# Two transformer blocks on one core: the attention heads and the second block's projections issued in a written order, and one PSUM bank for each branch product

## The chip, the cores and the metric

One core of a Trainium2 chip runs the whole program. Its engines work side by side from queues of their own: PE (TensorE, matrix products into PSUM), DVE (VectorE), ACT (ScalarE), POOL (GpSimd), and SP, which issues the transfers. The metric is the device time of one execution in microseconds (us), as the median of several.

## The reference

The input is one sequence of 256 tokens of width 1024, and everything is float32. The first model has two layers, each with a SwiGLU feed-forward, a mixer, and another feed-forward. The mixer of the second layer is a differential attention with 8 heads, whose keys and values come from the end of the first layer:

```python
    k, v = jnp.split(rms_norm(x, g_kv) @ w_kv, 2, axis=-1)
    ...
    q = (h @ w_q).reshape(b, s, N_HEADS, 2, HEAD_DIM) * (HEAD_DIM ** -0.5)
    ...
        scores = jnp.einsum("bqhcd,bkhcd->bhcqk", qb, k).astype(f32)
        ...
        p = jax.nn.softmax(jnp.where(causal, scores, -jnp.inf), axis=-1)
        a = p[:, :, 0] - lam * p[:, :, 1]
        return jnp.einsum("bhqk,bkhe->bqhe", a.astype(v.dtype), v)
    ...
    o = rms_norm(o, g_subln) * (1.0 - lambda_init)
    return o.reshape(b, s, D_MODEL) @ w_o
```

A second model follows. From the normalised tokens it projects the operands of two mixers: an HGRN2 recurrence with chunks of 64, and a sparse attention with rotary positions whose keys and values are compressed (32 tokens at a stride of 16, plus a position term, through a small two-layer network) and also used directly. The outputs of the two mixers are each multiplied by a branch weight and gated, added, and projected; a last feed-forward ends the program.

## The kernel before

**Precision and weights.** Each float32 operand is split into a high part and a remainder, so that one product is three matmuls (high by high, low by high, high by low). The weights arrive as 1 MB chunks in three `raw` buffers; the class `Stream` makes of each half chunk a high part (`hi()`, an ACT copy, line 194) and a remainder (`lo()`, a DVE subtraction, line 207) in ten pairs of slots `wh`, `wl`. `pump()` is one `hi` and one `lo`; `take` hands out halves in order; `done` frees a slot when its last matmul has been issued. Every matmul goes through the helper at line 430.

**Order.** Inside `with ordered():` the instructions of each engine stand in the order in which the code issues them. Outside it a scheduler chooses the order by priorities. Every engine works through its own instructions one after the other.

**PSUM.** `ps("acc")` has four banks of 128x512 float32, `ps("mm")` two and `ps("tr")` two.

**Ends of a feed-forward.** `Tail.close` accumulates the down projection, and between its rows it issues the next norm: `c2` the sum of squares, `c3a` and `c3b` the scaling (line 369) whose result PE transposes (line 416), and `fill`, the transposes and their splitting (lines 420 and 421). `close(ahead=2)` is that of the output projection of the attention, `close()` with `ahead=0` that of five other stages.

**Attention, 694 to 768 us.** For each head the scheduler gets: `att_kq` (k piece and q piece of 24 matmuls each, two `pump`s, two ACT copies to `kq`), `att_T(h-2)` (three transposes of the softmax result and one ACT copy, line 972), `att_scores(h)`, `att_av(h-2)` (three products with v into a `tr` bank, two ACT squares, then `rov` on DVE, a power on POOL, and the scaled result `gain` on DVE, line 988), and `att_soft(h)`. The last is on DVE two mask additions (line 944), which stand for `dg` in the texts, and four maxima (line 952); then four exponentials on ACT (line 955); then on DVE a reciprocal and five small products (lines 957 to 963), called the combination below. `v_part(1, 0)` and `v_part(1, 1)`, each 24 matmuls of 512 columns, stand ahead of heads 5 and 6. `att_out(pr)` transposes two heads' `gain` on PE (line 999) for the output projection `wo`, whose rows `wo.row` of six matmuls each stand in a written order from 768 us on, with the last heads' work between them.

**Projections of the second block, 992 to 1032 us.** `proj` is a product of 24 matmuls and one ACT copy (line 1086); `rope` is six small DVE operations; `dup_T` is two DVE copies (line 1111) and four transposes of their result. The sums of the compression (line 1153) read the transposed tokens `cT` and write `fT`, which the first product of `cmp_hidden` reads.

**Branch products, 1167 to 1186 us.** Eight products go to `acc` banks, two to each bank, and DVE multiplies each by its gate (line 1561).

Of the kernel before, what the change touches and what calls it, by code (L numbers as in the profile page):

```python
# [19 lines left out]
P = 128  # L20
T = 256
# [219 lines left out]
def tile_model(ctx: ExitStack, tc: tile.TileContext, w, wkv, x_in, gains, cst_in, pos_in, lbp, out):  # L241
# [334 lines left out]
    class Tail:  # L576
# [19 lines left out]
        def close(self, at=None, ahead=0):  # L596
# [5 lines left out]
            with ordered():  # L602
                for i in range(at, n):
                    self.row(0, i)
                self.row(1, rows[0])
                st.hi()
                bd.c2(0)
                bd.c3a(0)
                bd.c3b(0)
                for i in rows[1:5]:  # L610
                    self.row(1, i)
                    if i < rows[4]:
                        st.hi()
                st.lo()
                st.lo()
                bd.fill(0)
                for i in rows[5:-1]:
                    st.hi()
                    self.row(1, i)
                st.lo()  # L620
                st.lo()
                self.row(1, n - 1)
                bd.c2(1)
                bd.c3a(1)
                bd.c3b(1)
                while st.lo():
                    pass
# [283 lines left out]
    with ordered():  # L911
        v_part(0, 0)
        v_part(0, 1, {3: lambda: b4.fill(1)})
# [5 lines left out]
    def att_kq(h):  # L919
# [3 lines left out]
        st.pump(1)  # L923
        ws_piece(o[:, 1], ch, 1, qx)
        st.done(ch)
        kq = sb([P, 2, T], "opair", bufs=2)
        nc.scalar.activation(kq[:, 0], o[:, 0], AF.Copy)
        nc.scalar.activation(kq[:, 1], o[:, 1], AF.Copy, scale=0.125)
        st.pump(1)
        return kq  # L930

    def att_scores(h, kq):
# [73 lines left out]
    for h in range(8):  # L1006
        if h in (5, 6):
            v_part(1, h - 5)
        kq = att_kq(h)
        if h == 7:  # L1010
            att_out(0)
            att_out(1)
            b5.prep()
        if h >= 2:
            att_T(h - 2)
        sc = att_scores(h, kq)
        if h >= 2:
            att_av(h - 2)
        aa[h] = att_soft(h, sc)
# [16 lines left out]
    with ordered():  # L1036
        wo.row(0, 0)
        att_out(2)
        outs(2)
        wo.row(0, 1)  # L1040
        att_T(6)
# [46 lines left out]
    with ordered():  # L1088
        ch_1 = st.take(2)
        proj(bq[:, 0, 512:908], 0, ch_1, 396)  # L1090
        ch_q = st.take(2)
        proj(bq[:, 0, 0:512], 0, ch_q, 512, {5: lambda: b6.fill(1)})
        st.pump(2)
        proj(bq[:, 1, 512:908], 1, ch_1, 396)
        finish(ch_1)
        proj(bq[:, 1, 0:512], 1, ch_q, 512)
        finish(ch_q)
    ch_2 = st.take(2)
    for tb in range(2):
        rope(hd[:, tb, 0:10], tb, [P, 10, 8])  # L1100
        proj(bq[:, tb, 908:], tb, ch_2, 396)
    finish(ch_2)

# [13 lines left out]
    for tb in range(2):  # L1117
        rope(hd[:, tb, 12:20].rearrange("p (a b) d -> p a b d", b=4)[:, :, 0:2], tb, [P, 2, 2, 8])
    for tb in range(2):
        cs = slice(tb * P, (tb + 1) * P)  # L1120
        pt = ps("tr")
        for j in range(4):
            nc.tensor.transpose(pt[:, j * P:(j + 1) * P], bq[:, tb, j * P:(j + 1) * P], ident)
        pv = hv(pt)
        for i in range(2):
            nc.scalar.activation(qk_t[i][:, :, cs], pv[:, 2 * i:2 * i + 2], AF.Copy, scale=0.125)

    gates = sb([P, 2, 24], "gates")
    af = sb([P, 2, 512], "tmp", bufs=2)
    ch_f = st.take(2)  # L1130
    proj(af[:, 0], 0, ch_f, 512)
    for tb in range(2):
        cs = slice(tb * P, (tb + 1) * P)
        pv = dup_T(tb, (12, 16))
        for i in range(2):
            nc.scalar.activation(qk_t[2 + i][:, :, cs], pv[:, 2 * i:2 * i + 2], AF.Copy)
    proj(af[:, 1], 1, ch_f, 512)
    finish(ch_f)
    for tb in range(2):
        cs = slice(tb * P, (tb + 1) * P)  # L1140
        nc.scalar.activation(cT[:, :, cs], dup_T(tb, (8, 10)), AF.Copy)
    nc.scalar.activation(gates, bq[:, :, 1280:], AF.Sigmoid)
    nc.scalar.activation(af, af, AF.Sigmoid)
    ff = sb([P, D], "gain", bufs=2)
    fT = ff[:, :960].rearrange("p (s j g n) -> p s j g n", s=2, j=16, g=2)
    nc.gpsimd.memset(ff[:, 960:], 0.0)
    cv = cT.rearrange("p (s g) (n j e) -> p s j e g n", s=2, n=16, e=2)
    for s in range(2):
        for e in range(2):
            r = slice(e * 64, e * 64 + 64)  # L1150
            for hf in range(2):
                for g in range(2):
                    nc.vector.tensor_tensor(
                        fT[r, s, hf * 8:hf * 8 + 8, g],
                        cv[r, s, :, e, g, hf:hf + 15],
                        pe[r, s, hf * 8:hf * 8 + 8, None].to_broadcast([64, 8, 15]), op=OP.add)
# [603 lines left out]
```

## Time and profile before

| what | value |
|---|---|
| median of 3 runs | 1413.23 us (1412.24 to 1414.88) |
| the profiled execution's own time | 1413.44 us |
| its span, first to last instruction | 1411.4 us |
| mean granted clock of TensorE | 0.995 |
| PE busy | 1386.1 us (98%) |
| DVE busy | 873.3 us (62%) |
| ACT busy | 732.1 us (52%) |

The time of the execution holds 2.0 us outside the span. [...] A row of the timeline gives the start, the length, the instruction with its tiles (written <- read), how many were joined in the row, and in brackets how long the engine had been idle before it, with the instruction that ended the wait. Lengths of matmuls overlap in the pipeline, so the distance of two starts is what a matmul costs.

### The profile page before, as it was taken

What the parts mean: (1) busy time and instruction counts of PE and PEld (TensorE: products, weight loads), DVE (VectorE), ACT (ScalarE), POOL (GpSimd) and SP (SyncE); (2) the same over time, 40 slices, a digit from 0 to 9 for tenths busy, and PEclk for the clock granted to TensorE, in tenths of its full rate; (3) what the DMA queues carried; (4) which work ended last, traced back from release to release, by engine and by line L of the source; (5) the groups of instructions that cost most, each with busy time, mean ns of one, the idle gap of its engine ahead of it and who ended that gap; (6) DMA issues with size and microseconds to landing.
All of it is one profiled execution on the core that took longest, in us unless ns stands there. A gap on an engine that the chain in (4) does not pass through costs nothing.

```text
span 1411.4 us, 23060 instructions
## 1 busy us (share of the span) xinstructions
PE 1386.1 (98%) x9533; PEld 1268.7 (90%) x9533; DVE 873.3 (62%) x1358; ACT 732.1 (52%) x1216; POOL 32.3 (2%) x55
## 2 busy tenths in 40 slices
PE   8999999999999999999999999999999998999998
PEld 7999989999999899998898899998867998899996
DVE  5565576876555575654876765555679556675552
ACT  5454455455444454543665554444476954464451
POOL 0000000000000000000000000000000000000000
PEclk9999999999999999999999999999999999999999
DMA  7554556456555465554443465553653334355540
GB/s 272 204 201 179 185 226 216 176 183 222 196 179 179 151 237 184 208 191 150 154 175 134 151 246 186 183 186 112 234 228 120 120 135 161 123 211 207 183 146 30
DMA packets 38361, 252.93 MB, mean 179 GB/s; under 512 B 4328, under 2 KB 4720, under 8 KB 9968
## 3 DMA queue, kind: packets, MB, share of 16 engines
q1 hardware_dynamic: 37232, 250.20, 49.2%
q8 instruction: 75, 1.23, 0.3%
q10 hardware_dynamic: 1024, 1.25, 0.2%
q14 instruction: 30, 0.25, 0.0%
HBM read 250.39 MB, written 1.05 MB: 178 GB/s over the span
## 4 chain that ended last, share of the span: by engine, by line
PE 89%; DVE 5%; ACT 3%; issue 1%; DMA 1%; POOL 0%; ACTq 0%; POOLq 0%; DVEq 0%
PE mm L430 57%; PE acc L430 28%; PE tr L430 2%; DVE wl L207 2%; ACT wh L194 1%; PE tr L416 1%; PE tr L1300 0%; DVE x L351 0%; ACT junk L318 0%; DMA cst<-in_cst_dram 0%; POOL ssr L329 0%; DMA raw<-in_w_dram 0%; PE tr L554 0%; DVE tmp L340 0%; DVE ev L720 0%
## 5 line engine op out<-in xcount | busy, mean ns | idle before, releaser
L207 DVE TENSOR_TENSOR wl<-raw,wh 128x1024 fp32r<-128x1024 f32 (+1 forms) x454 | 539.6, 1213 | 189.4 <-ACT wh L194 186.3
L194 ACT ACTIVATE wh<-raw 128x1024 fp32r<-128x1024 f32 (+1 forms) x454 | 462.6, 1047 | 163.8 <-PE mm L430 87.8
L430 PE MATMUL mm<-xth,wh 128*128 128x256 f32 x1728 | 490.0, 284 | 0.6 <-DVE ev L1543 0.5
L430 PE MATMUL mm<-xth,wl 128*128 128x256 f32 x1728 | 487.8, 282 | 0.0
L430 PE MATMUL mm<-xtl,wh 128*128 128x256 f32 x1728 | 487.1, 282 | 0.0
L430 PE MATMUL acc<-wh,h 128*128 128x512 f32 x1120 | 352.7, 396 | 0.0
L430 PEld LDWEIGHTS mm<-xth,wh 128*128 128x128 f32 x1728 | 325.6, 188 | 3.3 <-DVE ev L1543 0.7
L430 PEld LDWEIGHTS mm<-xtl,wh 128*128 128x128 f32 x1728 | 326.0, 189 | 2.3 <-issue 0.5
L430 PEld LDWEIGHTS mm<-xth,wl 128*128 128x128 f32 x1728 | 325.2, 188 | 0.6 <-issue 0.5
L430 PEld LDWEIGHTS acc<-wh,h 128*128 128x128 f32 x1120 | 206.9, 188 | 46.1
L430 PE MATMUL acc<-wl,h 128*128 128x512 f32 x560 | 221.3, 395 | 0.0
L430 PE MATMUL mm<-wh,xth 128*128 128x256 f32 (+2 forms) x496 | 158.4, 319 | 1.9 <-ACT wh L194 1.7
L430 PE MATMUL mm<-wl,xth 128*128 128x256 f32 (+2 forms) x496 | 156.2, 315 | 1.6 <-DVE wl L207 1.4
L430 PE MATMUL mm<-wh,xtl 128*128 128x256 f32 (+2 forms) x496 | 156.6, 316 | 0.3 <-DVE xtl L421 0.3
L430 PEld LDWEIGHTS acc<-wl,h 128*128 128x128 f32 x560 | 105.2, 188 | 25.3
L560 ACT ACTIVATE ev<-mm 128x256 f32<-128x256 f32 x74 | 28.5, 385 | 165.1 <-PE mm L430 165.1
L430 PEld LDWEIGHTS mm<-wh,xth 128*128 128x128 f32 x496 | 94.4, 190 | 8.0 <-ACT wh L194 2.2
L430 PEld LDWEIGHTS mm<-wl,xth 128*128 128x128 f32 x496 | 94.2, 190 | 7.6 <-DVE wl L207 2.8
L430 PEld LDWEIGHTS mm<-wh,xtl 128*128 128x128 f32 x496 | 94.4, 190 | 4.9 <-DVE xtl L421 0.6
L561 DVE TENSOR_TENSOR ev<-ev,mm 128x256 f32<-128x256 f32 x74 | 31.1, 421 | 97.2 <-ACT ev L560 97.0
L458 ACT ACTIVATE h<-ev 128x256 fp32r<-128x256 f32 x106 | 44.3, 418 | 76.8 <-DVE ev L561 37.5
L459 DVE TENSOR_TENSOR h<-ev,h 128x256 fp32r<-128x256 f32 x106 | 45.1, 425 | 51.3 <-ACT h L458 51.3
(293 smaller groups left out, 918.3 us busy)
## 6 DMA issues: line engine op xcount, KB each, us to landing
raw<-in_w_dram SPq DMA_DIRECT2D x221, 1024.0 KB, 4.8
gain<-in_gains_dram SPq DMA_DIRECT2D x15, 512.0 KB, 4.8
raw<-in_wkv_dram SPq DMA_DIRECT2D x4, 792.0 KB, 4.8
wh<-in_w_dram SPq DMA_DIRECT2D x4, 512.0 KB, 9.0
wl<-in_w_dram SPq DMA_DIRECT2D x4, 512.0 KB, 10.3
x<-in_x_dram SPq DMA_DIRECT2D x2, 512.0 KB, 5.2
raw<-in_w_dram SPq DMA_DIRECT2D x2, 512.0 KB, 5.5
ev<-in_lbp_dram SPq DMA_DIRECT2D x1, 512.0 KB
```

Of the source, the lines that this page charges most:

```text
L194: self.nc.scalar.activation(h, r, AF.Copy)
L207: self.nc.vector.tensor_tensor(l, r, h.bitcast(F32), op=OP.subtract)
L416: nc.tensor.transpose(pt[:, j * P:(j + 1) * P], xn[:, k * P:(k + 1) * P], ident)
L430: nc.tensor.matmul(o, lhsT=a, rhs=b, start=start, stop=stop)
L458: last["act"] = nc.scalar.activation(dst[:, 0], src, AF.Copy).ins
L459: last["dve"] = nc.vector.tensor_tensor(dst[:, 1], src, dst[:, 0].bitcast(F32), op=OP.subtract).ins
L560: nc.scalar.activation(s, o[:, 0], AF.Silu)
L561: nc.vector.tensor_tensor(hf, s, o[:, 1], op=OP.mult)
```

## The change

Six places change. First, in `close` with `ahead=0` one of the two `lo` ahead of the last row moves to between `c3a(1)` and `c3b(1)`; with `ahead=2` the two `lo` ahead of the last row go behind it, one of them between `c3a` and `c3b`. Second, `b4.fill(1)` in `v_part(0, 1)` is issued at k=5 and not k=3. Third, the loop over the heads is written out inside `ordered()`, with the scores of a head in the next head's turn, and its product with v three turns on. Fourth, the rows of `wo` get the scores of head 7 and the rest in another order, and the loading of the Silu table is asked for by a small activation. Fifth, the projections, `rope`, the transposes and the sums of the compression stand in one `ordered()` block; the sums are 8 operations of 64x240 where there were 16 of 64x120, and are issued ahead of the last projection. Sixth, each branch product has an `acc` bank of its own.

```diff
                 for i in rows[5:-1]:
                     st.hi()
                     self.row(1, i)
-                st.lo()
-                st.lo()
+                if ahead == 0:
+                    st.lo()
+                    st.lo()
                 self.row(1, n - 1)
+                if ahead:
+                    st.lo()
                 bd.c2(1)
                 bd.c3a(1)
+                st.lo()
                 bd.c3b(1)
...
-        v_part(0, 1, {3: lambda: b4.fill(1)})
+        v_part(0, 1, {5: lambda: b4.fill(1)})
...
-    for h in range(8):
-        if h in (5, 6):
-            v_part(1, h - 5)
-        kq = att_kq(h)
-        if h == 7:
-            att_out(0)
-            att_out(1)
-            b5.prep()
-        if h >= 2:
-            att_T(h - 2)
-        sc = att_scores(h, kq)
-        if h >= 2:
-            att_av(h - 2)
-        aa[h] = att_soft(h, sc)
+    with ordered():
+        for h in range(8):
+            if h in (5, 6):
+                v_part(1, h - 5)
+            att_k(h)
+            if h >= 3:
+                att_av(h - 3)
+            if h >= 1:
+                aa[h - 1] = att_soft(h - 1, att_scores(h - 1))
+            if h >= 6:
+                att_out(h - 6)
+            att_q(h)
+            if h >= 2:
+                att_T(h - 2)
+        b5.prep()
...
         wo.row(0, 0)
+        aa[7] = att_soft(7, att_scores(7))
+        att_av(5)
+        wo.row(0, 1)
+        att_T(6)
         att_out(2)
         outs(2)
-        wo.row(0, 1)
-        att_T(6)
         wo.row(0, 2)
...
         wo.row(0, 4)
-        st.pump()
         att_av(7)
         wo.row(0, 5)
         wo.row(1, 0)
+        st.pump()
         att_out(3)
         outs(3)
+        nc.scalar.activation(warm, half[:, :1], AF.Silu)
         wo.row(1, 1)
...
+        ch_2 = st.take(2)
+        for tb in range(2):
+            cs = slice(tb * P, (tb + 1) * P)
+            rope(hd[:, tb, 0:10], tb, [P, 10, 8])
+            proj(bq[:, tb, 908:], tb, ch_2, 396)
+            if tb:
+                finish(ch_2)
+            pt = ps("tr")
+            for j in range(4):
+                nc.tensor.transpose(pt[:, j * P:(j + 1) * P], bq[:, tb, j * P:(j + 1) * P], ident)
...
+            nc.scalar.activation(cT[:, :, cs], dup_T(tb, (8, 10)), AF.Copy)
...
+        proj(af[:, 0], 0, ch_f, 512)
+        for s in range(2):
+            for e in range(2):
+                r = slice(e * 64, e * 64 + 64)
+                for hf in range(2):
+                    js = slice(hf * 8, hf * 8 + 8)
+                    nc.vector.tensor_tensor(fT[r, s, js], cv[r, s, :, e, :, hf:hf + 15],
+                                            pe[r, s, js, None, None].to_broadcast([64, 8, 2, 15]), op=OP.add)
+        for tb in range(2):
+            cs = slice(tb * P, (tb + 1) * P)
+            pv = dup_T(tb, (12, 16))
...
+        proj(af[:, 1], 1, ch_f, 512)
+        finish(ch_f)
+        nc.scalar.activation(gates, bq[:, :, 1280:], AF.Sigmoid)
+        nc.scalar.activation(af, af, AF.Sigmoid)
+        nc.scalar.activation(warm, half[:, :1], AF.Exp)
...
-                ob = ps("acc").rearrange("p (m t) -> p m t", m=2)
+            ob = ps("acc")[:, :T]
...
-            branch(ob[:, m % 2], brs[m // 2], m % 2, yb_h, yb_l, 1)
-            nc.vector.tensor_tensor(mgs[m][:, 1], mgs[m][:, 1], ob[:, m % 2], op=OP.mult)
+            branch(ob, brs[m // 2], m % 2, yb_h, yb_l, 1)
+            nc.vector.tensor_tensor(mgs[m][:, 1], mgs[m][:, 1], ob, op=OP.mult)
```

**Where instructions stand now, three places.** The first is DVE in the attention around `v_part(1, 1)`. Before, the mask additions of head 5 (L944), its first maxima, and `rov` and `gain` of head 3 stand between remainders `wl`:

```order
L207 TENSOR_TENSOR wl_7875<-raw_7558,wh_7874 128x1024
L207 TENSOR_TENSOR wl_7879<-raw_7558,wh_7878 128x1024
L944 TENSOR_TENSOR acc_7807<-acc_7807,cst_71 128x256
L207 TENSOR_TENSOR wl_7885<-raw_7666,wh_7884 128x1024
L944 TENSOR_TENSOR acc_7808<-acc_7808,cst_71 128x256
L952 TENSOR_REDUCE nm_7829<-acc_7807 128x1
L286 TENSOR_SCALAR rov_7821<-oss_7817 128x2
L952 TENSOR_REDUCE nm_7829<-acc_7807 128x1
L988 TENSOR_TENSOR gain_7208<-tr_7813,ror_7822 128x256
L952 TENSOR_REDUCE nm_7829<-acc_7808 128x1 x2
L207 TENSOR_TENSOR wl_7889<-raw_7666,wh_7888 128x1024
```

Now the last remainder of head 5's turn, those issued once `v_part(1, 1)` has freed its slots, and the first of head 6's turn stand ahead of `rov` and `gain` of head 3, and these stand ahead of the mask additions (L954 there) of head 5:

```order
L207 TENSOR_TENSOR wl_7797<-raw_7450,wh_7796 128x1024
L207 TENSOR_TENSOR wl_7834<-raw_7558,wh_7833 128x1024
L207 TENSOR_TENSOR wl_7838<-raw_7558,wh_7837 128x1024
L207 TENSOR_TENSOR wl_7844<-raw_7666,wh_7843 128x1024
L207 TENSOR_TENSOR wl_7848<-raw_7666,wh_7847 128x1024
L207 TENSOR_TENSOR wl_7879<-raw_7800,wh_7878 128x1024
L286 TENSOR_SCALAR rov_7890<-oss_7886 128x2
L998 TENSOR_TENSOR gain_7208<-tr_7882,ror_7891 128x256
L954 TENSOR_TENSOR acc_7895<-acc_7895,cst_71 128x256
L954 TENSOR_TENSOR acc_7896<-acc_7896,cst_71 128x256
L962 TENSOR_REDUCE nm_7904<-acc_7895 128x1 x2
```

Six `wl` in a row are ahead of `gain`, and the mask additions come last. The second place is DVE at the start of `wo`. Before, `gain` of head 5 (the second gain tile) stands ahead of the combination of head 7:

```order
L944 TENSOR_TENSOR acc_8091<-acc_8091,cst_71 128x256
L944 TENSOR_TENSOR acc_8092<-acc_8092,cst_71 128x256
L952 TENSOR_REDUCE nm_8113<-acc_8091 128x1 x2
L952 TENSOR_REDUCE nm_8113<-acc_8092 128x1 x2
L286 TENSOR_SCALAR rov_8105<-oss_8101 128x2
L988 TENSOR_TENSOR gain_7209<-tr_8097,ror_8106 128x256
L957 RECIPROCAL smr_8123<-sm_8114 128x4
L959 TENSOR_SCALAR rl_8125<-smr_8123,neglam_88 128x4
L962 TENSOR_SCALAR ev_8110<-ev_8110,rl_8125 128x256
L962 TENSOR_SCALAR ev_8110<-ev_8110,rl_8125 128x128
L963 SCALAR_TENSOR_TENSOR tmp_8127<-ev_8110,smr_8123 128x256
L963 SCALAR_TENSOR_TENSOR tmp_8127<-ev_8110,smr_8123 128x128
```

Now it stands behind the combination of head 7, and `out(2)` on PE reads it:

```order
L954 TENSOR_TENSOR acc_8099<-acc_8099,cst_71 128x256
L954 TENSOR_TENSOR acc_8100<-acc_8100,cst_71 128x256
L962 TENSOR_REDUCE nm_8108<-acc_8099 128x1 x2
L962 TENSOR_REDUCE nm_8108<-acc_8100 128x1 x2
L967 RECIPROCAL smr_8118<-sm_8109 128x4
L969 TENSOR_SCALAR rl_8120<-smr_8118,neglam_88 128x4
L972 TENSOR_SCALAR ev_8105<-ev_8105,rl_8120 128x256
L973 SCALAR_TENSOR_TENSOR tmp_8122<-ev_8105,smr_8118 128x256
L972 TENSOR_SCALAR ev_8105<-ev_8105,rl_8120 128x128
L973 SCALAR_TENSOR_TENSOR tmp_8122<-ev_8105,smr_8118 128x128
L286 TENSOR_SCALAR rov_8135<-oss_8131 128x2
L998 TENSOR_TENSOR gain_7209<-tr_8127,ror_8136 128x256
```

What moved is `rov` and `gain` of head 5, past the reciprocal and the five products behind it. The third place is DVE in the second block's projections, at the copies of `dup_T(tb, (8, 10))`, which are the last two `COPY` rows of before:

```order
L1080 TENSOR_TENSOR big_10318<-junk_10581 128x2x2x8
L1081 TENSOR_TENSOR big_10318<-junk_10581 128x2x2x8
L1111 COPY opair_10640<-big_10318 128x256 x2
L1111 COPY opair_10696<-big_10318 128x256 x2
L1111 COPY opair_10705<-big_10318 128x256 x2
L207 TENSOR_TENSOR wl_10560<-raw_10429,wh_10559 128x1024
L207 TENSOR_TENSOR wl_10564<-raw_10429,wh_10563 128x1024
```

Now two remainders stand between `rope` of the second 128 tokens and the copy for them:

```order
L1092 TENSOR_TENSOR junk_10540<-big_10319,cos_92 128x80
L1093 TENSOR_TENSOR junk_10540<-big_10319,sin_91 128x80
L1094 TENSOR_TENSOR big_10319<-junk_10540 128x10x8
L1095 TENSOR_TENSOR big_10319<-junk_10540 128x10x8
L207 TENSOR_TENSOR wl_10582<-raw_10435,wh_10581 128x1024
L207 TENSOR_TENSOR wl_10586<-raw_10435,wh_10585 128x1024
L1109 COPY opair_10598<-big_10319 128x256 x2
```

The remainders that stood behind all the copies are now ahead of the one that PE's transposes wait for.

## Rows read from the trace of the kernel before

**Rows 1.** Page, part 1: busy us, share of the span, instructions of each engine.

```profile
PE 1386.1 (98%) x9533; PEld 1268.7 (90%) x9533; DVE 873.3 (62%) x1358; ACT 732.1 (52%) x1216; POOL 32.3 (2%) x55
```

**Rows 2.** Busy time by engine in three stretches; clock, DMA share, GB/s.

```profile
694.50:768.00 73.50, 72.18 (x558) 66.92 (x557) 56.41 (x126) 49.79 (x129) 3.50 (x5) 1.00 0.52 192
768.00:795.00 27.00, 26.34 (x132) 21.32 (x131) 15.06 (x33) 15.44 (x41) 3.21 (x5) 1.00 0.18 59
...
1167.00:1186.00 19.00, 14.44 (x117) 13.59 (x116) 9.31 (x15) 6.87 (x9) 0.00 (x0) 1.00 0.47 172
```

**Rows 3.** Timeline of PE, attention heads and output projection: start, length, instruction, wait.

```profile
714.10 0.49 PE L971 MATMUL tr<-cst,tmp 128*128 128x128 f32 x3
...
721.88 0.49 PE L971 MATMUL tr<-cst,tmp 128*128 128x128 f32 x3
...
768.05 0.71 PE L430 MATMUL mm<-wh,h 128*128 128x512 f32 x2
...
769.53 0.38 PE L999 MATMUL tr<-cst,gain 128*128 128x128 f32 x2
```

**Rows 4.** Timeline of DVE, one attention head.

```profile
725.06 0.76 DVE L944 TENSOR_TENSOR acc<-acc,cst 128x256 f32<-128x256 f32 x2
...
726.59 0.15 DVE L286 TENSOR_SCALAR rov<-oss 128x2 f32<-128x2 f32 x1
...
727.56 0.42 DVE L988 TENSOR_TENSOR gain<-tr,ror 128x256 f32<-128x256 f32 x1 [0.62 <-POOL ror L287]
728.13 0.18 DVE L957 RECIPROCAL smr<-sm 128x4 f32<-128x4 f32 x1
...
729.73 1.22 DVE L207 TENSOR_TENSOR wl<-raw,wh 128x1024 fp32r<-128x1024 f32 x1
```

**Rows 5.** Timeline of ACT, one attention head.

```profile
722.93 0.36 ACT L927 ACTIVATE opair<-mm 128x256 f32<-128x256 f32 x1
...
723.46 0.49 ACT L972 ACTIVATE tmp<-tr 128x384 f32<-128x384 f32 x1
...
726.37 0.47 ACT L955 ACTIVATE ev<-acc,nm 128x256 f32<-128x256 f32 x1 [0.23 <-DVE nm L952]
...
727.98 1.07 ACT L194 ACTIVATE wh<-raw 128x1024 fp32r<-128x1024 f32 x1
```

**Rows 6.** Timeline of PE, four waits at the ends of feed-forwards and projections.

```profile
690.06 1.06 PE L416 MATMUL tr<-cst,tmp 128*128 128x128 f32 x8 [0.35 <-DVE tmp L369]
...
805.35 1.06 PE L416 MATMUL tr<-cst,tmp 128*128 128x128 f32 x8 [0.66 <-DVE tmp L369]
...
807.52 0.39 PE L430 MATMUL mm<-wl,xth 128*128 128x256 f32 x1 [0.76 <-DVE wl L207]
...
996.08 0.50 PE L430 MATMUL mm<-wl,xth 128*128 128x512 f32 x1 [0.45 <-DVE wl L207]
```

**Rows 7.** Timeline of ACT, second block's projections.

```profile
1018.21 0.50 ACT L1086 ACTIVATE big<-mm 128x396 f32<-128x396 f32 x1 [3.85 <-PE mm L430]
1018.65 1.21 ACT L1126 ACTIVATE h<-tr 128x256 f32<-128x256 f32 x4
1019.88 1.28 ACT L1142 ACT_TABLE_LOAD   x1
```

**Rows 8.** Timeline of DVE, second block's projections.

```profile
1011.19 2.35 DVE L207 TENSOR_TENSOR wl<-raw,wh 128x1024 fp32r<-128x1024 f32 x2
...
1019.60 0.49 DVE L1111 COPY opair<-big 128x256 f32<-128x256 f32 x2
```

**Rows 9.** Timeline of PE, start of the compression.

```profile
1035.96 1.07 PE L430 MATMUL mm<-wh,gain 128*32 128x256 f32 x4 [2.92 <-DVE gain L1153]
```

**Rows 10.** One-microsecond stretches behind that start; the column after POOL is the clock.

```profile
1036.00:1037.00 1.00, 1.00 (x5) 0.19 (x5) 0.99 (x5) 0.00 (x0) 0.00 (x0) 0.50 1.00 401
...
1039.00:1040.00 1.00, 1.00 (x14) 0.42 (x16) 0.97 (x4) 0.00 (x0) 1.00 (x2) 0.84 1.02 418
```

**Rows 11.** Chain of waits, first branch products.

```profile
1168.90 1.22 DVE wl L207
1170.12 0.34 DVE h L1561
```

More of the change, by code (lines that the diff above doesn't have):

```diff
@@ L917, in tile_model, with att_k @@
     opairs = {i: opair_t[i // 2][:, i % 2] for i in range(4)}
-    def att_kq(h):
+    kqs = {}
+    def att_k(h):
         ch = st.take()[0]
@@ L922, in att_kq, with att_q, att_scores @@
         ws_piece(o[:, 0], ch, 0, kvt)
-        st.pump(1)
+        kqs[h] = ch, o
+        st.pump()
+    def att_q(h):
+        ch, o = kqs[h]
         ws_piece(o[:, 1], ch, 1, qx)
         st.done(ch)
-        kq = sb([P, 2, T], "opair", bufs=2)
+        kq = kqs[h] = sb([P, 2, T], "opair", bufs=2)
         nc.scalar.activation(kq[:, 0], o[:, 0], AF.Copy)
         nc.scalar.activation(kq[:, 1], o[:, 1], AF.Copy, scale=0.125)
-        st.pump(1)
-        return kq
-    def att_scores(h, kq):
+        st.pump()
+    def att_scores(h):
+        kq = kqs[h]
         sc = [ps("acc") for _ in range(2)]
@@ L1050, in tile_model @@
         wo.row(1, 0)
+        st.pump()
         att_out(3)
         outs(3)
+        nc.scalar.activation(warm, half[:, :1], AF.Silu)
         wo.row(1, 1)
@@ L1086, in proj @@
         nc.scalar.activation(dst, o[:, :n], AF.Copy)
[L1088 to L1102, printed above, removed]
     qk_t = [sb([P, 2, T], "h", bufs=HB) for _ in range(4)]
@@ L1115, in dup_T @@
         return hv(pt)
[L1117 to L1156, printed above, removed]
+    with ordered():
+        ch_1 = st.take(2)
+        proj(bq[:, 0, 512:908], 0, ch_1, 396)
+        ch_q = st.take(2)
+        proj(bq[:, 0, 0:512], 0, ch_q, 512, {6: lambda: b6.fill(1)})
+        st.pump(2)
+        proj(bq[:, 1, 512:908], 1, ch_1, 396)
+        finish(ch_1)
+        proj(bq[:, 1, 0:512], 1, ch_q, 512)
+        finish(ch_q)
+        ch_2 = st.take(2)
[8 more added lines that the diff above has]
+                nc.tensor.transpose(pt[:, j * P:(j + 1) * P], bq[:, tb, j * P:(j + 1) * P], ident)
+            pv = hv(pt)
+            for i in range(2):
+                nc.scalar.activation(qk_t[i][:, :, cs], pv[:, 2 * i:2 * i + 2], AF.Copy, scale=0.125)
+            nc.scalar.activation(cT[:, :, cs], dup_T(tb, (8, 10)), AF.Copy)
+        gates = sb([P, 2, 24], "gates")
+        af = sb([P, 2, 512], "tmp", bufs=2)
+        ch_f = st.take(2)
+        for tb in range(2):
+            rope(hd[:, tb, 12:20].rearrange("p (a b) d -> p a b d", b=4)[:, :, 0:2], tb, [P, 2, 2, 8])
+        ff = sb([P, D], "gain", bufs=2)
+        fT = ff[:, :960].rearrange("p (s j g n) -> p s j g n", s=2, j=16, g=2)
+        nc.gpsimd.memset(ff[:, 960:], 0.0)
+        cv = cT.rearrange("p (s g) (n j e) -> p s j e g n", s=2, n=16, e=2)
+        proj(af[:, 0], 0, ch_f, 512)
[6 more added lines that the diff above has]
+                                            pe[r, s, js, None, None].to_broadcast([64, 8, 2, 15]), op=OP.add)
+        for tb in range(2):
+            cs = slice(tb * P, (tb + 1) * P)
+            pv = dup_T(tb, (12, 16))
+            for i in range(2):
+                nc.scalar.activation(qk_t[2 + i][:, :, cs], pv[:, 2 * i:2 * i + 2], AF.Copy)
+        proj(af[:, 1], 1, ch_f, 512)
[3 more added lines that the diff above has]
+        nc.scalar.activation(warm, half[:, :1], AF.Exp)
```

## The prediction

> **What bounds the kernel now.** I read the engines' busy time first: PE works 1386.1 of 1411.4 us, DVE 873.3 and ACT 732.1 [rows 1]. So PE sets the end; a change can win only some of PE's 25 us without work (and the stretches at half clock), and loses wherever it makes PE wait anew. Then I read the stretches that the change touches: PE is idle 73.50 - 72.18 = 1.32 us in the attention and 0.66 us at the start of the output projection, about 2.0 in both, and 4.56 us in the branch products [rows 2]. Then the timeline of PE for what ends each wait, and those of DVE and ACT for what stands ahead of that instruction. An idle time in brackets is counted from the modelled end of a matmul, and a matmul of 256 columns lasts 0.28 where the next starts 0.12 later, so I count 0.16 on top for each wait that goes.
>
> **Branch products: -5.2.** The second product of a bank waits until DVE has multiplied the first, since DVE reads the bank that PE is to write. DVE is late because a remainder stands ahead, 1168.90 to 1170.12, and the multiplication ends 0.34 later [rows 11]. There are four such waits, 4.56 us in all [rows 2], and with 4 x 0.16 that is 5.2. With a bank for each product PE needs, four products on, a bank that DVE has long read, so nothing is late next but the weights; their remainders come one in a pair of products, 24 matmuls at 0.12 or 2.8 us, and take 1.22 on DVE and 1.07 on ACT [rows 4, 5], which both fit.
>
> [...]
>
> **Closes and the earlier fill: -2.7.** At the end of the output projection PE waits 0.66 for the scaling and 0.76 for a remainder [rows 6]. With the scaling ahead of the two `lo` and the Silu table asked for earlier, both are early: -1.4 - 2 x 0.16 = -1.7. At 996.08 the 0.45 wait for a remainder goes in the same way, -0.6; at 690.06 the transposes come 1.4 us later, behind two more of the section's steps, and their 0.35 wait goes, -0.35. In the other four closes one `lo` of 1.22 merely changes places with scalings; PE has a row of six matmuls before it there, 1.48 [rows 3], and I take nothing.
>
> **Attention: +7.8.** One head takes PE 721.88 - 714.10 = 7.78 [rows 3]. In the written order DVE and ACT have a circle of their own. Count from the first exponential of a head, a. ACT: exponentials until a + 1.61 (727.98 - 726.37), `kq` 0.53 (723.46 - 722.93), `hi` 1.07, the copy of the transposes 0.49, ended at about a + 3.6, then a second `hi` to a + 4.6 [rows 5]. DVE: reciprocal at a + 1.76 (728.13 - 726.37), combination ended at a + 3.36 (729.73 - 726.37), then `lo`, then the second `lo`, which waits for the second `hi`, to a + 5.7. Only now `rov`, through POOL to `gain` 0.97 later (727.56 - 726.59), then the mask additions at a + 7.1, and from them to the next exponential 1.31 (726.37 - 725.06) [rows 4, 5]: 8.4 us, where starts overlap by 0.1 as two `lo` in 2.35 do [rows 8]. Before, the mask additions stood ahead of `rov` and the remainders where the operands came that way; now 8.4 has to fit into 7.78 and doesn't.
>
> What is late is the copy of the transposes, and with it the product with v one piece later. Early heads: 0.8 and 0.5 of wait, from the start of the circle. `v_part(1, 0)` and `v_part(1, 1)` give PE 24 matmuls of 512 columns more each, 5.6 us (six take 1.48 at most [rows 3]), so the circle catches up. Behind `v_part(1, 1)` (its end is V) five `hi` and five `lo` stand ahead of `gain` of head 3: the first `hi` ends at V + 1.7, five `lo` at 1.13 (2.35 - 1.22) each end at V + 7.4; `gain` and the mask additions of head 5 are at V + 8.7, their exponentials at V + 10.0, the transposes' copy for head 4 ends 3.6 later and behind an output copy of 0.6, at V + 14.2. PE wants it at V + 11.2 to 11.9: a wait of 2.3 to 3.0. The next circle, 8.4 + 0.6, puts the exponentials of head 6 at V + 19.0, `kq` of head 7 at V + 21.7, and its mask additions, behind the scores and a `lo`, at V + 24.1. The combination ends 1.31 + 3.36 later, V + 28.8, and only behind it stand `rov` and `gain` of head 5, ended at V + 30.2. `out(2)` waits for that. PE's own work from V is two heads, 15.56, two outputs of about 0.45, two rows of 1.48 [rows 3], and the scores, product and transposes of a head, 7.78 less two pieces of 2.84: 21.5 us. So 8.7 of wait lie in this chain, the last 4 of them at `out(2)`; with 1.3 before it 9.9, less the 2.1 that PE waits there now. The bounds: nothing new where the circle hides (-2.1), and 11 with `hi` and `lo` at full length without overlap.
>
> [...]
>
> **Second block's projections: +2.2.** The stall of 2.92 at the compression [rows 9] goes, since its sums are done a projection earlier: -3.1; behind it PE runs at 0.50 from 1036 until within 1039 to 1040 [rows 10], some 3.4 us in which half the work is done: -1.7; a wait of about 0.5 near it goes too. In return: the transposes of the first 128 tokens wait 0.65 for `rope` behind remainders. `finish(ch_2)` puts two `hi` and two `lo` ahead of the copy for `dup_T`: from E, the last matmul of the projection at 1018.0, the ACT copy ends near E + 0.65 [rows 7], `hi` at E + 1.7, two `lo` 2.35 later, the copies 0.49 [rows 8]: E + 4.2 to 4.5, and PE has 0.45 of other transposes, so it waits 3.8. Then the exponentials of the sparse attention stand behind four more `hi` and two table loads of 1.28 [rows 7]: 1.2 and 2.0 at two transposes. 7.6 - 5.4 = +2.2. Bounds: -5.4 if the remainders come when PE is busy elsewhere, and +4 with both table loads in full.
>
> **The clock.** One long wait of PE, 2.92 with little work ahead of it, was followed by the clock at 0.50, at 1.7 us; the waits in the branch products, 4.56 in four, were followed by none: the stretch stands at 1.00 [rows 2, 9, 10]. The new waits at `out(2)` (4) and at `dup_T` (3.8) are longer than 2.92, so I count two such drops, +3.4; those of 2 to 3 us lie between the two rows, and I count none (bound: +3.4 more, or none at all).
>
> [...]
>
> **Sum:** -5.2 - 2.7 + 7.8 + 2.2 + 3.4 = +5.5, by rows of an execution of 1413.44, which is 0.2 over the median of 1413.23. So 1418.7 for the median.
>
> **Rivals.** *Faster: the circle is hidden.* If the circle is under 7.78 (one `lo` fewer ahead of `rov`, 1.13, decides it), or the `hi` behind V come while PE is in the section so that the clump is done sooner, only the gains count: -5.2 - 2.7 - 2.1, and in the projections, with the remainders late and harmless, about -3: -13, 1400. For it speaks that DVE and ACT are idle a quarter of the attention's time [rows 2]; against it, that the chain V to `out(2)` is of dependent steps, which idle engines don't shorten. Chance 0.17. *Half the attention's waits and one drop:* -3.9 - 1.7 from the sum, 1413.1. Chance 0.17. *The same waits without a drop of the clock:* 1415.3. Chance 0.15. *More drops:* four in place of two, 1422. Chance 0.08. *The branch waits stay*, because the weights are late instead, chained as they are to PE's release of slots: +5.2, 1424. Chance 0.04; the chain shows a remainder whose ACT copy was itself late [rows 11]. That the order isn't kept is no rival: it is written out and stands so in the program.
>
> **How the numbers follow.** The forecast, 1417 to 1420.5, has 0.39. A difference of 0.2% is 2.8 us, about what a measurement of this kernel can tell from no change: faster is below 1410.4, slower above 1416.1. Faster holds the hidden circle and a quarter of the half case: 0.21. Same holds the rest of the half case and two thirds of the dropless one: 0.23. The rest is slower: 0.56. The range leaves out most of the hidden circle and the branch case: 1406 to 1423. If only the forecast's case is meant, it is 1417 to 1420.5.
>
> **What would show it.** Right: PE waits of 2 to 4 us ahead of the product of head 4 and of `out(2)`, released by `gain`; one near 4 us ahead of `dup_T`, released by a COPY behind two `wl`; no wait for line 1561's product; the clock at 0.50 behind the long waits. Wrong: PE idle under 3 us from 694 to 795, or heads 7.8 us apart with `gain` on time; then the circle had slack that I missed, and the time ends near 1400 to 1410.

## The result: 0.57% slower, and the profile after

The changed kernel takes 1421.69 us (median of 6 runs, 1421.06 to 1423.68), the kernel before 1414.34 (6 runs); the ratio is 1.0057, 95% interval 1.0045 to 1.0069, or 8.1 us (6.4 to 9.8). One execution each of experiments 1 and 3 below took 5085 and 5741 us; the ratios leave it out. The profiled execution of the changed kernel took 1422.28 us, its span is 1420.5, its granted clock 0.991. The granted clock is the share of full speed that TensorE was given; the lowest share in the traces of the two kernels is 0.50, called half clock.

Counting PE's instructions, which are as many as before, the same place in the program is reached so much later than in the trace of before:

| up to | later by, us | in this stretch |
|---|---|---|
| start of the first section of v | 1.08 | +1.08 |
| first k piece (694.46 before) | 0.53 | -0.54 |
| end of the output projection's close (808) | 10.62 | +10.08 |
| second block's first projections (1009) | 9.90 | -0.73 |
| middle of the sparse attention (1075) | 14.65 | +4.76 |
| branch products (1167.7) | 14.66 | 0.0 |
| behind them (1187) | 9.10 | -5.57 |
| end | 9.04 | -0.06 |

The first line is no part of the change: a load of constants landed 5.3 us after its issue in place of 4.2, and one remainder came 0.76 late at 80 us. In the twelve profiles below that place is between 1.2 us earlier and 1.8 us later than in the trace of before, so single profiles carry that much, and the ratios are used for times.

The page, the stretches that answer to [rows 1, 2], and the waits of PE by releaser (us in total, times, longest):

```profile
PE 1390.7 (98%) x9533; PEld 1273.7 (90%) x9533; DVE 874.7 (62%) x1350; ACT 732.1 (52%) x1218; POOL 38.2 (3%) x55
```

```profile
694.50:768.00 73.50, 68.97 (x519) 63.82 (x518) 51.28 (x108) 45.14 (x116) 3.02 (x5) 0.99 0.44 159
768.00:810.00 42.00, 37.40 (x193) 30.79 (x192) 25.07 (x58) 22.27 (x59) 3.68 (x6) 0.90 0.30 109
1167.00:1195.00 28.00, 28.00 (x241) 27.88 (x240) 17.11 (x24) 14.95 (x20) 1.01 (x1) 1.00 0.48 173
```

```profile
PE tr L1112 <- DVE opair L1109: 3.8, 1, 3.8
PE tr L430 <- ACT tmp L982: 3.4, 3, 1.9
PE tr L1009 <- ACT tmp L982: 2.1, 1, 2.1
PE tr L1009 <- DVE gain L998: 2.1, 1, 2.1
...
PE tr L1186 <- ACT ct L1183: 1.4, 1, 1.4
...
PE tr L981 <- DVE gain L998: 1.1, 1, 1.1
```

PE is busy 4.6 us more for the same number of matmuls; more of them ran at half clock: 17.0 us at 0.50 between 20 and 1400 us, against 3.4 before. Line 1561's waits (4.56 before) are gone, and the branch products' stretch has no idle time at all. In their place stand the wait for the copy of `dup_T` and six waits on the attention's `tmp` and `gain`. On PE's timeline (what answers to [rows 3, 6]):

```profile
714.12 0.49 PE L981 MATMUL tr<-cst,tmp 128*128 128x128 f32 x3
...
718.34 0.94 PE L430 MATMUL tr<-big,tmp 128*128 128x128 f32 x6 [0.89 <-ACT tmp L982]
...
723.00 0.49 PE L981 MATMUL tr<-cst,tmp 128*128 128x128 f32 x3
...
726.91 0.94 PE L430 MATMUL tr<-big,tmp 128*128 128x128 f32 x6 [0.57 <-ACT tmp L982]
...
731.57 0.49 PE L981 MATMUL tr<-cst,tmp 128*128 128x128 f32 x3
...
759.85 0.52 PE L981 MATMUL tr<-cst,tmp 128*128 128x128 f32 x3 [1.13 <-DVE gain L998]
...
765.16 0.94 PE L430 MATMUL tr<-big,tmp 128*128 128x128 f32 x6 [1.94 <-ACT tmp L982]
...
779.61 0.44 PE L1009 MATMUL tr<-cst,gain 128*128 128x128 f32 x2 [2.13 <-ACT tmp L982]
782.13 0.69 PE L1009 MATMUL tr<-cst,gain 128*128 128x128 f32 x2 [2.08 <-DVE gain L998]
...
1034.17 1.09 PE L1112 MATMUL tr<-cst,opair 128*128 128x128 f32 x4 [3.79 <-DVE opair L1109]
```

Heads are 8.88 and 8.57 apart (714.12, 723.00, 731.57) where they were 7.78. The clock in stretches of 2 us, in the column behind POOL (the third half-clock stretch answers to [rows 10]):

```profile
766.00:768.00 2.00, 2.00 (x12) 1.63 (x12) 1.63 (x3) 0.68 (x5) 0.23 (x1) 0.57 0.43 66
768.00:770.00 2.00, 2.00 (x12) 2.00 (x11) 1.49 (x5) 0.00 (x0) 0.47 (x1) 0.58 0.82 336
...
780.00:782.00 2.00, 0.04 (x1) 0.00 (x0) 1.09 (x5) 0.00 (x0) 0.70 (x1) 0.50 0.00 0
782.00:784.00 2.00, 1.87 (x6) 1.58 (x7) 0.50 (x2) 0.69 (x1) 0.00 (x0) 0.50 0.00 0
784.00:786.00 2.00, 2.00 (x8) 1.71 (x7) 0.32 (x1) 0.00 (x0) 0.00 (x0) 0.50 0.00 0
786.00:788.00 2.00, 2.00 (x11) 1.70 (x10) 0.17 (x1) 0.63 (x4) 0.28 (x1) 0.81 0.00 0
...
1032.00:1034.00 2.00, 0.00 (x0) 0.00 (x0) 2.00 (x4) 0.92 (x3) 0.00 (x0) 0.63 1.00 385
1034.00:1036.00 2.00, 1.83 (x7) 1.67 (x8) 1.80 (x15) 0.60 (x1) 0.00 (x0) 0.50 1.03 424
...
1038.00:1040.00 2.00, 2.00 (x7) 1.56 (x6) 1.97 (x5) 0.00 (x0) 0.00 (x0) 0.67 1.05 424
```

Between 20 and 1400 us there are three stretches at 0.50: about 3.4 us from 766.3, 6.8 from 779.9 and 6.8 from 1032.5. In the two long ones PE still waits at first, so that it works for 3.4, 4.7 and 5.2 us at 0.50; if half as much is done in that time, they cost an estimated 1.7, 2.4 and 2.6 us. A matmul of 512 columns starts 0.43 us after the one before from 1035.48 to 1038.89, and 0.23 from 1039.56 to 1040.96, so a little more than half was done and the estimate is some 10% high. On DVE, what stands ahead of the copy for `dup_T`:

```profile
1031.45 2.36 DVE L207 TENSOR_TENSOR wl<-raw,wh 128x1024 fp32r<-128x1024 f32 x2 [5.50 <-ACT wh L194]
1033.73 0.49 DVE L1109 COPY opair<-big 128x256 f32<-128x256 f32 x2
...
1035.92 4.21 DVE L1155 TENSOR_TENSOR gain<-ev,cst 64x240 f32<-64x240 f32 x8
```

### The profile page after: what moved, and what is told of

Its sections match the earlier page's. It is cut to its first block, busy times and chain, and to the rows that moved or that the text cites. A ratio compares the mean times of both kernels' runs of the same rounds, so it can differ in the third digit from the quotient of the medians.

```text
span 1420.5 us, 23038 instructions
## 1 busy us (share of the span) xinstructions
PE 1390.7 (98%) x9533; PEld 1273.7 (90%) x9533; DVE 874.7 (62%) x1350; ACT 732.1 (52%) x1218; POOL 38.2 (3%) x55
## 4 chain that ended last, share of the span: by engine, by line
PE 86%; DVE 6%; ACT 4%; issue 1%; DMA 1%; POOL 1%; ACTq 0%; POOLq 0%; DVEq 0%
PE mm L430 55%; PE acc L430 27%; DVE wl L207 2%; PE tr L430 2%; ACT wh L194 2%; PE tr L416 1%; ACT ev L965 1%; POOL ssr L329 0%; PE tr L1310 0%; DMA posi<-in_pos_dram 0%; DMA cst<-in_cst_dram 0%; DVE x L351 0%; PE tr L554 0%; DMA raw<-in_w_dram 0%; DVE acc L954 0%
## 5 line engine op out<-in xcount | busy, mean ns | idle before, releaser
L561 DVE TENSOR_TENSOR ev<-ev,mm 128x256 f32<-128x256 f32 x74 | 31.2, 422 | 97.2 <-ACT ev L560 97.0
## 6 DMA issues: line engine op xcount, KB each, us to landing
wl<-in_w_dram SPq DMA_DIRECT2D x4, 512.0 KB, 10.1
```

What stands on the lines that cost most here:

```text
L561: nc.vector.tensor_tensor(hf, s, o[:, 1], op=OP.mult)
```

## Experiments

Times are medians of 4 to 11 runs; each ratio is to the runs of the kernel before on the same chip (medians 1413.3 to 1413.64). 0.1% is 1.4 us. Differences to the changed kernel are those of the ratios. The granted clock differs between executions of one kernel (0.992 to 0.996 in run 4), and a trace shows one of them.

**1. The old attention, the rest changed.** The loop over the heads and the rows of `wo` are those of before.

> The changed kernel with the attention loop and the rows of the output projection of before (the scheduler's order), all else changed. Theory (the written order of the attention costs its waits and two half-clock stretches): the 10.1 us that the changed kernel's trace loses between the first k piece and the end of the output projection are gone, and about 0.5 to 1.5 of the close's gain stays, so 10 to 11 us below the changed kernel, 1410.5 to 1412, 3 us below before. Rival (the loss belongs to the later fill or to the close): within 3 us of the changed kernel.

Measured: 1409.94 us, ratio 0.9975 (0.9966 to 0.9984), 11.6 us below the changed kernel by the ratios. The loss is the written order of the attention and the first rows of `wo`; close and fill gain (1.3 and 0.5 us in this trace).

**2. The old projections, the rest changed.**

> The changed kernel with the second block's projections and compression sums as before. Theory (dup_T's wait for the copy behind two remainders and the half-clock stretch cost more than the vanished 2.92 us stall gave): 3.5 to 5 us below the changed kernel, 1417 to 1418, with the 2.92 us stall back. Rival (the written projections are a gain and the loss lies in the attention alone): the same or up to 3 us above the changed kernel.

Measured: 1417.04, ratio 1.0022 (1.0013 to 1.0031), 4.9 below the changed kernel. From 1018 to 1115 this trace keeps the same distance to before's within 0.02 us, with the stall back, 2.93 us.

**3. Matmuls that nobody reads in two of the waits.**

```diff
+    def filler(n, a):
+        o = ps("acc")[:, :T]
+        for _ in range(n):
+            mm(o, a[:, :P], a, True, True)
...
         for j in range(4):
+            if idle and j % 2 == 0:
+                filler(17, idle)
             nc.tensor.transpose(pt[:, j * P:(j + 1) * P], op[:, j], ident)
...
+            if tb:
+                filler(30, xt.H(0))
             nc.scalar.activation(cT[:, :, cs], dup_T(tb, (8, 10)), AF.Copy)
```

> The changed kernel with matmuls whose result nobody reads in PE's two longest waits: 17 of 256 columns ahead of each half of out(2), 30 ahead of dup_T of the second 128 tokens; the waits themselves and their causes stay. Theory (the half-clock stretches behind these waits follow from PE's idling and cost 2.4 and 2.6 us): clock 1.00 behind both, 4 to 5 us below the changed kernel, about 1417; the stretch at 766 to 770, which gets no filler, stays. Rival (the clock falls for another reason, or the stretches cost nothing because PE waits there anyway): within 1 us of the changed kernel, or slower by the filler.

Measured: 1418.17, ratio 1.0032 (1.0020 to 1.0044), 3.5 below the changed kernel. The same stretches of its trace:

```profile
766.00:768.00 2.00, 2.00 (x13) 1.50 (x12) 1.94 (x3) 1.00 (x5) 0.00 (x0) 0.59 0.15 33
...
780.00:782.00 2.00, 2.00 (x18) 2.00 (x19) 1.09 (x5) 0.00 (x0) 0.70 (x1) 1.00 0.01 4
782.00:784.00 2.00, 1.95 (x12) 1.53 (x11) 0.75 (x2) 0.69 (x1) 0.00 (x0) 1.00 0.03 8
...
1034.00:1036.00 2.00, 2.00 (x10) 1.64 (x9) 1.99 (x5) 0.00 (x0) 0.00 (x0) 1.00 1.05 426
...
1038.00:1040.00 2.00, 1.40 (x8) 0.69 (x7) 1.92 (x5) 0.60 (x1) 1.10 (x1) 1.00 1.04 432
```

Behind both fillers the clock stands at 1.00; at 766 to 770, where there was none, it is down as before. PE has more to do and still ends earlier, so here the half clock follows from the idling and costs. The gain is under the 4 to 5 expected, by the new idle time at 1038 to 1040 (0.60): PE, faster now, reaches the next copies before the sums are done.

**4. Remainders later on DVE.** PE's order is kept.

```diff
@@ att_k, att_q
-        st.pump()
+        st.hi()
@@ att_soft
+        st.lo()
         r = sb([P, 4], "smr", bufs=2)
...
+        st.lo()
         return at
```

Behind the second section of v the freed slots are only released, and the last two chunks of `wo` are taken ahead of `row(0, 4)`.

> The changed kernel with the order of PE kept, and the remainders moved on DVE: one lo between the maxima and the reciprocal, one behind the combination, so that one fewer stands ahead of rov, gain and the mask additions; the four conversions that the second v section frees are spread over the following heads, and the last two chunks of the output projection are taken four rows later. Theory (the circle of 8.4 us and the clump of remainders make the waits): heads 7.8 us apart, waits under 3 us from the first k piece to out(2), no half clock there: 8 to 10 us below the changed kernel, 1412 to 1414. Rival (scores one piece later and the product with v three turns on make the waits, whatever stands between on DVE): within 3 us of the changed kernel.

Measured: 1418.19 (1415.59 to 1421.30), ratio 1.0030 (1.0019 to 1.0041): 3.8 below the changed kernel, less than half of what was expected. The trace is of an execution of 1415.89. On PE's timeline:

```profile
711.88 0.49 PE L986 MATMUL tr<-cst,tmp 128*128 128x128 f32 x3
...
719.60 0.49 PE L986 MATMUL tr<-cst,tmp 128*128 128x128 f32 x3
...
758.38 0.83 PE L430 MATMUL tr<-big,tmp 128*128 128x128 f32 x6
...
773.88 0.44 PE L1014 MATMUL tr<-cst,gain 128*128 128x128 f32 x2 [1.67 <-ACT tmp L987]
777.53 0.69 PE L1014 MATMUL tr<-cst,gain 128*128 128x128 f32 x2 [3.21 <-DVE gain L1003]
```

Heads stand 7.72 apart without a wait, and nothing waits ahead of the product of head 4: circle and clump together were what made the early waits. The run moves copies (`hi`) of the clump too, so it doesn't tell these from the remainders. But `row(0, 0)` waits 1.68 for the bank that head 7's `kq` is read from, and `out(2)` 1.67 and 3.21, since `gain` of head 5 still stands behind the softmax of head 7. The clock falls to 0.50 twice, from 767.1 and from 777.4, for 3.4 us each. The theory holds for the heads and fell for the end.

**5. The product of head 5 ahead of the softmax of head 7.** In the changed kernel `att_av(5)` moves up one line.

> The changed kernel with one step moved: the product of head 5 with v (and with it its rov and gain) ahead of the scores and the softmax of head 7. Theory (out(2) waits 2.1 for gain of head 5 because that stands behind the softmax of head 7, and the clock halves behind that wait): the second wait at out(2) gone, but about 1 us of new wait for the copy of head 5's transposes; 2 to 5 us below the changed kernel, 1417 to 1419. Rival (out(2) is late because everything behind the v section is late): within 1.5 us of the changed kernel.

Measured: 1417.12, ratio 1.0029 (1.0018 to 1.0039), 4.0 below the changed kernel: the 2.13 and 2.08 at `out(2)` are gone, new waits of 0.36 and 0.97 stand at products with v, and the clock is 1.00 in every stretch from 768 to 790. One line was worth as much as experiment 4's rearrangement.

**6. `finish(ch_2)` behind `dup_T`.**

> The changed kernel with finish(ch_2), two hi and two lo, issued behind dup_T of the second 128 tokens and not ahead of it. Theory (the two remainders alone make the 3.8 us wait, and the wait the half clock): the wait at dup_T under 1 us, clock 1.00 behind it, 5 to 6 us below the changed kernel, 1416. Rival (the wait only moves on: the sums, or the scaled exponentials, stand behind the same remainders now): a new wait of 2 to 4 us further on and 0 to 2 us gained.

Measured: 1422.90, ratio 1.0065 (1.0052 to 1.0077): nothing gained; the rival was the nearer one. DVE and then PE of its trace:

```profile
1032.44 2.36 DVE L207 TENSOR_TENSOR wl<-raw,wh 128x1024 fp32r<-128x1024 f32 x2 [6.06 <-ACT wh L194]
...
1036.31 4.10 DVE L1154 TENSOR_TENSOR gain<-ev,cst 64x240 f32<-64x240 f32 x8
1040.44 1.72 DVE L1109 COPY opair<-big 128x256 f32<-128x256 f32 x4
```

```profile
1030.11 0.60 PE L1112 MATMUL tr<-cst,opair 128*128 128x128 f32 x4
...
1040.88 0.66 PE L1112 MATMUL tr<-cst,opair 128*128 128x128 f32 x2 [4.58 <-DVE opair L1109]
```

The first `dup_T` now runs at once (1030.11), but the copies for the next one stand behind the same two remainders and the eight sums, 4.10 us: PE waits 4.58, and the clock falls to 0.50 during that, at 1039.0, for 6.8 us. In the changed kernel PE, held up earlier, reached the copies behind the sums only when the sums were done.

**7. The banks of the branch products alone, on the kernel before.**

> The kernel before with one part of the change, a bank for each branch product. Theory: the four waits go and nothing takes their place, 5.2 to 5.6 us below before, 1408 (ratio 0.996). Rival (the weights are late instead): within 1.5 us of before.

Measured: 1408.12, ratio 0.9965 (0.9952 to 0.9977): -5.5 us by the medians, -4.9 by the ratio, about as expected. Its trace loses nothing elsewhere, and the stretch of the branch products is 5.57 us shorter.

**8. Close, fill and banks, on the kernel before.**

> The kernel before with the three parts that order neither the attention nor the projections: the moved remainders in the closes, the later fill and the banks of the branch products. Theory (the parts add up as they do in the trace: -0.5 fill, -1.3 close, -0.7 projections' first wait, -5.6 banks): 8 us below before, 1405.5 (ratio 0.9943). Rival (a part works only with the written orders): less than 6 us.

Measured: 1405.44, ratio 0.9945 (0.9933 to 0.9958): -8.2 us against before by the medians, -7.8 by the ratio. The parts add up.

**9. As 6, and the sums behind the copies.** Beside the edit of run 6 two loops change places: `dup_T(tb, (12, 16))` and its copies first, the eight sums behind.

> The changed kernel with finish(ch_2) behind dup_T of the second 128 tokens, as in the run in which the wait only moved, and the eight sums of the compression behind the copies of dup_T(tb, (12, 16)) and ahead of the last projection. Theory (whatever stands on DVE ahead of a copy that PE's transposes need makes the wait: first two remainders, then 4.1 us of sums): no wait above 1 us at any dup_T, no half clock behind, 5 to 6.5 us below the changed kernel, 1415.5 to 1417. Rival (the last projection and its conversions are late in any order): a wait of over 2 us at the sums' reader or at the exponentials, under 2 us gained.

Measured: 1415.47, ratio 1.0009 (1.0001 to 1.0018), 6.8 below the changed kernel. No `dup_T` waits over 0.5; from 1030 to 1045 the clock is 1.00 and PE busy 14.54 us, where the changed kernel shows 0.77 and 11.21:

```profile
1030.00:1045.00 15.00, 14.54 (x84) 11.80 (x82) 8.96 (x27) 6.08 (x13) 1.43 (x2) 1.00 0.88 347
```

```profile
1030.00:1045.00 15.00, 11.21 (x47) 9.10 (x46) 10.17 (x28) 5.22 (x11) 1.63 (x2) 0.77 0.84 324
```

So the 3.8 us and the half clock with it were `finish(ch_2)`, the two remainders and the copies they wait for, and, once that was moved, the sums.

**10. The three parts of 8 and the projections of 9, the attention as before.**

> The three parts and the mended projections together, the attention as before. Theory (parts add up; the mended projections are 4.5 - 6.3 = 1.8 us below those of before): 1403 to 1404.5, ratio 0.993, and so below the kernel before and the changed one. Rival (the mended projections are only level with before's): 1405.5.

Measured: 1405.22, ratio 0.9934 (0.9921 to 0.9948). It beats both kernels. Against run 8 it is 0.2 us lower by the medians and 1.6 by the ratios, whose intervals overlap, so its times don't show the mended projections to be better than the old ones. The traces do, by 0.9 us: counted as in the table above, the stretch from 990 to 1075 is, against the kernel before, 1.65 us shorter in runs 9, 10 and 11, which have the mended ones, and 0.7 shorter in runs 2 and 8, which have the old ones.

**11. Both written orders mended.** Attention of 4, with 5's line and `out(2)` two rows later, projections of 9.

> The attention in a written order with the remainders later, the product of head 5 with v ahead of the softmax of head 7 and out(2) two rows later, and the mended projections. Theory (the order of PE that the change wrote is good where DVE's own order doesn't hold it up): waits from the first k piece to the end of the output projection under 2.5 us in sum, no half clock, 1401 to 1404. Rival (one piece later is too late for the last heads in any case): waits of 4 us or more there and a time above the run with the attention as before.

Measured: 1412.12, ratio 0.9990 (0.9981 to 0.9999): above run 10, as the rival said. The waits moved again: 3.59 at 783.54 ahead of the transposes of head 7 (behind `out(2)`'s copies), 1.68 and 1.60 ahead of it, and the clock falls to 0.50 at the end of the 3.59, from 783.3 for 3.4 us.

**12. The old loop in a written order.** Run 1 with its loop inside `ordered()`.

> The run with the attention of before and all else changed, with one edit: the loop of before, statement for statement, inside ordered(), so that its scores follow their q piece at once and nothing is moved up by the scheduler. It tells apart whether the changed attention loses by being in a written order at all, or by the order that was written. Theory A (a written order is worth only what DVE and ACT allow; the scheduler of before moved scores and maxima to where their operands were): PE waits 0.6 to 0.9 for kq ahead of each head's scores and for the copy of the transposes ahead of the product with v, some 8 to 12 us in all, 1418 to 1422. Theory B (scores one piece later and the last heads' order are the fault): within 2 us of the run with the scheduler's order, 1410 to 1412.

Measured: 1419.10, ratio 1.0045 (1.0029 to 1.0062), 9.9 above run 1 by the ratios. Its waits of PE:

```profile
PE acc L430 <- ACT opair L932: 4.1, 7, 0.7
...
PE tr L975 <- DVE h L1006: 3.6, 1, 3.6
PE tr L430 <- ACT tmp L976: 2.0, 5, 0.4
```

Seven of its scores wait for `kq` (0.6 on average), five products for the transposes. Theory A holds in the time: the same statements cost 10 us more once their order is fixed, with scores at once as with scores one piece later. It named the 4.1 and the 2.0 us; the 3.6 us wait, ahead of the transposes of a late head, it did not. The granted clock of the profiled execution is 0.994, where run 1's is 0.998.

## Why the prediction was right, step by step

The time, 1421.69, lies in the range of 1406 to 1423, near its upper end, and the direction was the likelier one. It is 3.0 above the forecast of 1418.7, outside the forecast's own case of 1417 to 1420.5, and next to the 1422 of the rival "more drops", which had a chance of 0.08. As a change, +5.5 us was forecast and +8.1 measured. By its steps:

**Branch products, -5.2.** Measured -5.57 in the trace and by themselves -5.5 by the medians (run 7). Shown: with a bank for each product the four waits of 4.56 us went, and nothing took their place.

**Closes and fill, -2.7.** Measured -0.54 for the fill, -0.73 at 996, and -1.28 at the close of `wo` (run 8's trace, where the attention is that of before): -2.55. Shown for the three together; only the last is a little under -1.7, as in run 8 a wait of 0.21 for a remainder is left at 806.09. In the closes with `ahead=0` the `lo` that moved came from behind `c3b(1)`, and not from the two ahead of the last row: those two stay (996.32 and 997.46 on DVE), and one now stands at 1003.82, ahead of the scaling at 1005.49. In the projections `b6.fill(1)` moved as well, from k=5 to k=6; runs 2 and 8, where it didn't, gain the same 0.7 at 996.

**Attention, +7.8.** The waits were forecast as 0.8 and 0.5 early, 2.3 to 3.0 behind V, and about 4 at `out(2)`. Measured: 0.89 and 0.57, then 1.13 + 1.94 = 3.07, then 2.13 + 2.08 = 4.21, 8.7 in all against 9.9, or 9.7 with the prediction's 0.16 on top for each of six. The dates hold as well. A circle lasts 8.50 us (first exponentials of two heads at 723.26 and 731.76), against 8.4. With V at 750.9 the five remainders end at V + 7.4, the mask additions start at V + 8.7, and the copy of the transposes ends at V + 14.2, all as forecast; `gain` of head 5 ends at V + 31.2 in place of 30.2:

```profile
723.26 0.47 ACT L965 ACTIVATE ev<-acc,nm 128x256 f32<-128x256 f32 x1 [3.32 <-DVE nm L962]
...
731.76 0.47 ACT L965 ACTIVATE ev<-acc,nm 128x256 f32<-128x256 f32 x1 [3.20 <-DVE nm L962]
```

```profile
752.56 5.77 DVE L207 TENSOR_TENSOR wl<-raw,wh 128x1024 fp32r<-128x1024 f32 x5 [3.13 <-ACT wh L194]
...
759.62 0.75 DVE L954 TENSOR_TENSOR acc<-acc,cst 128x256 f32<-128x256 f32 x2
...
781.65 0.42 DVE L998 TENSOR_TENSOR gain<-tr,ror 128x256 f32<-128x256 f32 x1 [0.88 <-POOL ror L287]
```

```profile
764.57 0.53 ACT L982 ACTIVATE tmp<-tr 128x384 f32<-128x384 f32 x1
```

That the circle and the clump make the early waits is shown by run 4, that the place of `gain` of head 5 makes the last by run 5. Three things in the prediction don't fit. Its sum is 0.2 off: 8.7 + 1.3 is 10.0, and the waits of before are 1.32 + 0.66 = 2.0, which makes +8.0. Of its 8.7 us from V only 2.3 to 3.0 and 4 have a place in the program; 7.3 were measured. Last, not all these waits end with `gain`: the 1.94 ahead of the product of head 4 ends with the copy of the transposes, and the first 2.13 at `out(2)` with that of head 6, which stands on ACT behind the exponentials of head 7. On DVE `rov` and `gain` of head 3, at 758.24 and 759.28, come behind all five remainders (752.56 to 758.33). The prediction saw one thing too narrowly: the `lo` ahead of `rov` are one cause, but mending them (runs 4, 11) only moves the waits to the last heads. Their chain from scores to `out` seems longer than the rows of `wo` put between; no run changes that alone.

**Projections, +2.2.** The wait at `dup_T` was forecast as 3.8 and is 3.79, the one for `rope` 0.65 and is 0.81; the two at the exponentials 1.2 and 2.0, measured 0.69 and 1.38. The cause of the 3.79 is shown by runs 6 and 9. The other three stand in run 9 too (0.82, 0.69, 1.39); their causes are read from the trace and not tested. The 0.69 comes behind four `hi` (3.89 us) and two table loads of 1.28, as forecast, the 1.38 behind a copy of PSUM (`ct`) that follows four more `hi` (3.93). The stall of 2.92 and its half clock went as said. With the new half clock the stretch lost 4.76, against 2.2 + 1.7.

**The clock, +3.4.** This term was mis-sized: measured, by the estimate above, 1.7 + 2.4 + 2.6 = 6.7. Two stretches of some 3.4 us were counted; there are three, and two of them last 6.8. The third stands behind waits of 1.13 and 1.94, each shorter than the 2.92 that the prediction took as its row. Nor does it take two: in run 4 a single wait of 1.68 at 766.20 was followed by 3.4 us at 0.50 from 767.1, while in run 11 the same wait of 1.68 at 769.13 left the clock at 1.00, in every stretch from 752 to 782. So the length of a wait alone doesn't decide. Waits that were counted right so cost more: the attention's stretch with its close lost 10.1 us in place of 7.8 - 1.7 + 1.7 = 7.8, and that is most of what the forecast lacks. Run 3 shows that filling two of the waits gives back 3.5 us.

**The rivals.** The hidden circle fell: the circle lasts 8.50 against 7.78, and runs 1 and 12 show that a fixed order costs 10 to 12 us here. "More drops" was the case nearest to what happened (three, not four). The order was kept, and the branch waits did not stay.

The same 3.79 us wait at `dup_T` is followed by 6.8 us at 0.50 in the changed kernel and by 3.4 in run 1. The traces show one difference: in the changed kernel the clock falls at 1032.5, 1.7 us before PE's work comes back, in run 1 at 1023.1, 0.85 behind its return at 1022.29:

```profile
1022.00:1024.00 2.00, 1.71 (x8) 1.51 (x9) 1.90 (x15) 0.60 (x1) 0.00 (x0) 0.78 1.02 420
```

It is so in other traces too. The stretches of 6.8 us at 779.9 in the changed kernel and at 1039.0 in run 6 began 2.2 and 1.9 us before the end of PE's wait (782.13 and 1040.88). Those of 3.4 us began at most 0.2 before it (1035.9 in before, 777.4 in run 4, 783.3 in run 11) or up to 1.1 behind it (766.3 in the changed kernel, 767.1 in run 4). So how much a wait cost was in part luck that the sum could not hold. Open: what sets the moment at which the clock falls. No run here tells that.

## What to carry to other kernels

Before fixing the order of a loop that a scheduler has laid out, follow each queue for one period and add up what stands ahead of an instruction on its engine, conversions of later weights above all. Here the chain's period was 8.50 us against 7.78 on PE, and PE waited at its last consumers: 0.89 and 0.57 at the early products with v, later 1.94 there and 2.13 and 2.08 at `out(2)`. With the remainders later (run 4) heads stood 7.72 apart. Count a long wait of TensorE with the half-clock stretch that can follow it, as a range and not as one figure: here 3.4 or 6.8 us followed the same wait, and waits of 1.68 and 1.94 us were followed by one of 3.4 (run 4, the changed kernel), another of 1.68 by none (run 11). Parts of a change should be timed apart: here three small ones gave 8 us and two large ones took 16.

## What the runs showed of the hardware that was not expected

The eight sums of 64x240 take 4.21 us on DVE (from 1035.92 in the changed kernel), 526 ns each, where sixteen of 64x120 took 4.61, one every 288: half the instructions saved 0.4 us. A wait of 1.94 us behind one of 1.13 was followed by 3.4 us at half clock, and in run 4 one of 1.68 alone, while the four waits of 0.78 to 1.36 in before's branch products, one in 4.3 to 4.9 us, left the clock at 1.00 [rows 2].
